# Half of q as a pair of seven products, the first pair's weights in places of their own, and a third group ahead of the last heads

## The chip, the cores and the metric

One Trainium2 chip, of which the kernel uses one core. The metric is the device time of one execution in microseconds. The engines are called as in the profile: PE (TensorE: matmuls, with PEld for its weight loads), DVE (VectorE), ACT (ScalarE), POOL (GpSimd) and SP (SyncE, which only issues DMAs). Each works through its own instructions in order; instructions on different engines meet through semaphores.

## What is computed

One layer of an encoder on 1024 tokens of 1024 channels, all in float32. The input is normalised, then one projection of 1024 x 5120 gives eight parts:

```python
h = layer_norm(x, emb_ln_g, emb_ln_b)
q, k, v, z_a, u, z_b, g_a, g_b = split(h @ w_in)          # 4 x 512, 2 x 512, 2 x 1024
attn = neighbourhood_attention(q, k, v, rpb)              # 8 heads of 64, window 8 x 16 on a 16 x 64 grid
y_a = attn * silu(z_a)
u = centred_depthwise_conv(u, conv_w, conv_b)
y_b = (rg_lru(u, forward) + rg_lru(u, backward)) * silu(z_b)
m = sigmoid(g_a + b0) * (y_a @ w_ba) + sigmoid(g_b + b1) * (y_b @ w_bb)
out = layer_norm(ALPHA * h + m @ w_out)
```

## The kernel before

**Products in three parts.** Every float32 operand of a matmul is split into a high half (rounded to the type that PE takes) and a low half (the rest). `mm3` (line 122) makes a product of three matmuls for each piece of 128 of the inner dimension: high x high, low weight x high, high weight x low. The high half is a copy, mostly on ACT, the low half a difference (`lo_of`, line 119) on DVE or POOL.

**Stage 1, lines 369 to 559.** Eight tiles of 128 tokens are loaded, normalised, turned by PE (`tile_in`) and split into the four blocks B11, B12, B21, B22 (inner dimension by token half). v is computed tile by tile (`v_part`, `v_hi`, `v_lo`, `v_store`). For the later tiles (4 to 7) the sums T1 to T4 of blocks are formed: `t_full` (line 271: a copy t3 by ACT out of PSUM, then four differences on DVE), `t_last` (line 282, two more), `t_hi` (ACT) and `t_lo` (POOL).

**q, lines 508 to 582.** q has 512 channels, so four blocks m of 128, each in two token halves n. `q_part(m, n)` is a plain product of 24 matmuls; `qk_load` and `qk_prep` load and split its weights (high on ACT, low on POOL); `q_hi`, `q_lo`, `q_store` scale it by 0.125, split it and send it to DRAM. (0, 0) and (1, 0) stand among the tiles; the other six run after the last v, in the loop of line 561. In that loop the weights of pair 0 are loaded (`s_load`), summed (`s_sum`, DVE) and split (`s_hi`, `s_lo`).

**The pair loop, lines 973 to 1001.** k, z_a, z_b, u, g_a and g_b are computed two blocks of 128 channels at a time: 16 pairs, each a 2 x 2 product of blocks in seven products of 12 matmuls (the sums a11, a12, s2, s1, s3, s4, a22 of weight blocks against B11, B21, T2, T1, T3, B22, T4) in place of eight. One product is a slot. In slot k of a pair the results of earlier products leave PSUM (`evacuate`, line 896: ACT's copies u1, u2, u3 and DVE's sums, through the `take_...` function of that pair), and one operand of the next pair is prepared. `at(slot, pos, f)` puts other work in slots by hand: the convolution stages at `CONV_AT`, two gate stages and a scan for each of four channel blocks at `GATE_AT`, the pools of the next stage at `LATE_AT` and `HEAD_AT`. PE gets four small matmuls of a gate stage in between. The decay rates (lines 594 to 612) are some 30 tiny steps on DVE ahead of the loop.

**Attention, lines 1145 to 1210.** Head by head scores, softmax and values, with the y_b branch product as filler matmuls.

**Merge and output, lines 1225 to 1339.** The y_a branch products (`b_group`, 12 matmuls for a group, three for each k, where k is a pair of heads) run slot by slot. The last pair of heads (k = 3) is finished late by `gated` (DVE, ACT, DVE). So the groups of slots 0 and 1 run their first three k, and the two fourths follow in slot 1. `merge` and `merge_lo` combine both branches and split the sum; then come the output products (`o_product`) and the last normalisation.

What sets the order: all five queues are written out by hand (`manual_schedule`), so the program's order is the order of each engine. Buffers of one tag are shared, and a new tile waits until the old one's readers are done.

Of the kernel before, what the change touches and what calls it, by code (L numbers as in the profile page):

```python
# [14 lines left out]
P = 128  # L15
# [51 lines left out]
def encoder_kernel(ctx, tc, x, gb1, gb, w_qk, w_v, w_s, w_ba, w_bb, w_gate, smalls, bias, w_out, out):  # L67
# [35 lines left out]
    V.memset(eps_z[:], EPS * TWICE * TWICE)  # L103
    smh = cst.tile([P, SM_N], F32, name="smh")
    warm = cst.tile([P, 1], F32, name="warm")
# [13 lines left out]
    def lo_of(eng, lo, full, hi):  # L119
        eng.tensor_tensor(lo, full, hi.bitcast(F32), ALU.subtract)  # L120
# [119 lines left out]
    def keep(i):  # L240
        SP.dma_start(h_d[i], xs[i][:])
# [12 lines left out]
    def tp4(i, kk):  # L254
        return tps[i, kk][:].rearrange("p (k t) -> p k t", k=4)
# [12 lines left out]
    def f(t, i):  # L268
        return t[:, :, ti(i)].bitcast(F32)

    def t_full(i):

        for c, tag in ((1, "a21"), (2, "a12"), (3, "a22")):
            tt[i, c] = wsp.tile([P, 4, P], F32, tag=tag, bufs=2 if c == 3 else 1, name=f"t{c}_{i}")
        t1, t2, t3 = (tt[i, c][:] for c in (1, 2, 3))
        A.copy(t3, tp4(i, 0))
        V.tensor_tensor(t1, tp4(i, 0), f(B11[0], i), ALU.subtract)
        V.tensor_tensor(t1, t1, f(B11[1], i), ALU.subtract)
        V.tensor_tensor(t2, tp4(i, 1), t1, ALU.subtract)
        V.tensor_tensor(t3, tp4(i, 1), t3, ALU.subtract)  # L280
# [6 lines left out]
    def t_hi(i, *cs):  # L287
        for c in cs:
            A.copy(Ts[c][0][:, :, ti(i)], tt[i, c][:])
# [53 lines left out]
    def s_load(p, *names):  # L343
        for o in names if p < N_PAIR else ():
            t = wsp.tile([P, 4, P], F32, tag=o, bufs=2 if o == "a22" else 1, name=f"{o}_{p}f")
            SP.dma_start(t[:], w_s[p, ("a11", "a21", "a12", "a22").index(o)])
            s_a[p, o] = t

    def s_sum(p, *names):
        for o in names if p < N_PAIR else ():  # L350
            a, b, op = dict(s1=("a21", "a22", ALU.add), s2=("s1", "a11", ALU.subtract),
                            s3=("a11", "a21", ALU.subtract), s4=("a12", "s2", ALU.subtract))[o]
            t = s_a[p, o] = wsp.tile([P, 4, P], F32, tag=o, name=f"{o}_{p}f")
            V.tensor_tensor(t[:], s_a[p, a][:], s_a[p, b][:], op)
# [141 lines left out]
    keep(5)  # L496
    qk_load(2)
    tile_in(4)
    tile_lo(4)
    ln_next(7)  # L500
    t_full(4)
    v_part(3, "a", KS)
# [14 lines left out]
    t_lo(4, 4)  # L517
    keep(7)
    q_part(1, 0)
    t_full(5)  # L520
    q_hi(1, 0)
# [37 lines left out]
    v_store(7)  # L559
    s_load(0, "a11")  # L560
    for m in range(4):
        for n in BOTH if m > 1 else (1,):
            q_part(m, n)
            if m < 2:
                qk_prep(m + 2)
                if m == 0:
                    qk_load(3)
                    t_hi(7, 2, 1, 3)
                    t_lo(7, 2, 1, 3)
                    t_last(7)  # L570
                    t_hi(7, 4)
                    t_lo(7, 4)
                    s_load(0, "a21", "a22", "a12")
                else:
                    s_sum(0, "s1", "s2", "s3", "s4")
            q_hi(m, n)
            q_lo(m, n)
            q_store(m, n)
            if m > 1:
                for w in (OPS[:2], OPS[2:4], OPS[4:6], OPS[6:])[2 * (m - 2) + n]:  # L580
                    s_hi(0, w)
                    s_lo(0, w)
    s_load(1, "a11", "a21", "a12", "a22")
    for pl in (ln, wpl, hb12, pst, ps0):
        pl.release()
# [7 lines left out]
    nsp = lru.tile([P, 8], F32, name="nsp")  # L593
    t0, t1, t2 = (lru.tile([P, 8], F32, name=f"sp{c}") for c in range(3))
    lam = sm[:, SM_LAM:SM_LAM + 8]
    V.tensor_scalar(smh[:], sm[:], 0.5, None, ALU.mult)
    V.tensor_scalar(t0[:], lam, -1.0, None, ALU.mult)
    V.tensor_tensor(t0[:], lam, t0[:], ALU.min)
    A.activation(t0[:], t0[:], AF.Exp)
    V.tensor_scalar(t1[:], t0[:], 2.0, None, ALU.add)  # L600
    V.reciprocal(t1[:], t1[:])
    V.tensor_tensor(t0[:], t0[:], t1[:], ALU.mult)
    V.tensor_tensor(t1[:], t0[:], t0[:], ALU.mult)
    V.tensor_scalar(t2[:], t1[:], 1.0 / 21.0, 1.0 / 19.0, ALU.mult, ALU.add)
    for n in (17, 15, 13, 11, 9, 7, 5, 3, 1):
        V.tensor_tensor(t2[:], t2[:], t1[:], ALU.mult)
        V.tensor_scalar(t2[:], t2[:], 1.0 / n, None, ALU.add)
    V.tensor_tensor(t2[:], t2[:], t0[:], ALU.mult)
    V.tensor_scalar(t0[:], lam, -1.0, 0.0, ALU.mult, ALU.max)
    V.scalar_tensor_tensor(t0[:], t2[:], 2.0, t0[:], ALU.mult, ALU.add)  # L610
    V.tensor_scalar(sp[:], t0[:], C_LRU, None, ALU.mult)
    V.tensor_scalar(nsp[:], t0[:], -C_LRU, None, ALU.mult)

# [36 lines left out]

    def take_k(m0):

        def consume(mi, n, add, o, c=None):
            c = o if c is None else c
            if add is not None:
                V.tensor_tensor(c[:], add[:], o[:], ALU.add)
            tag, w = ("uc", S) if (mi, n) == (1, 1) else ("up", S + 3)
            t = lru.tile([P, w], F32R, tag=tag, bufs=2, name=f"k{m0}{mi}{n}")
            hi, lo = t[:, :HALF], t[:, HALF:S]

            def high():
                A.copy(hi, c[:])

            def store():
                lo_of(V, lo, c[:], hi)
                SP.dma_start(k_d[m0 + mi][:, :, halves[n]], t[:, :S].rearrange("p (z f) -> p z f", z=2).bitcast(F32))
            return [high, store]
        return consume
# [134 lines left out]

    late, b_w, heads = {}, {}, {}

# [62 lines left out]
    def gates_a(j):  # L868
        return lambda: take_zg(ga_d, 2 * j, "ga", SM_BM)

    def gates_b(j):
        return lambda: take_zg(gb_d, 2 * j, "gb", SM_BM + 8)

    takes = [lambda: take_u(0), lambda: take_zg(zb_d, 0, "zb"), lambda: take_zg(za_d, 0, "za"), gates_a(0), gates_a(1),
             lambda: take_u(2), gates_b(0), lambda: take_zg(zb_d, 2, "zb"), gates_a(2), gates_b(1),
             lambda: take_k(0), gates_a(3), lambda: take_k(2), lambda: take_zg(za_d, 2, "za"), gates_b(2), gates_b(3)]
# [354 lines left out]
    for slot in range(2 * NK + 2):  # L1231
        j, n = divmod(slot, 2)
        if 1 < slot <= 2 * NK:
            merge(*divmod(slot - 1, 2), sums_m[slot - 1])
        if slot == 2:
            at0.release()
            mlp = pool("mlp")
            ml.update({(j, n): mlp.tile([P, HALF], F32R, name=f"ml{j}{n}") for j in range(NK) for n in range(2)})
            wo += [pair(mlp, [P, D], f"wo{k}") for k in range(NK - 2, NK)]
        for q in (0, 1) if slot == 2 else (slot - 2,) if slot > 3 else ():  # L1240
            merge_lo(*divmod(q, 2), sums_m.pop(q))
        if slot == 2:
            pst.release()
            banks[0] = tc.alloc_tile_pool(name="ps8", bufs=8, space=bass.MemoryType.PSUM, reuse_waits="tile")
        if j < NK:
            if n == 0:
                b_load(0, j + 2)
            g_load(0, j + 1, n, **(dict(tag=f"u{slot % 4}", bufs=1) if slot % 4 else dict(tag="z", bufs=5)))
            o = sums_m[slot] = pst.tile([P, HALF], F32, tag="mb", bufs=2, name=f"mb0{n}") if slot < 2 else bank(f"mb{j}{n}")
# [6 lines left out]
            if n == 0 and j > 0:  # L1256
                b_split(0, j + 1, A)
# [168 lines left out]
```

## Time and profile before

| | us |
|---|---|
| median of 3 runs | 686.44 |
| lowest, highest | 683.94, 686.56 |
| profiled execution, its time | 684.15 |
| profiled execution, its span | 682.4 |
| mean granted TensorE clock | 0.996 |

The span goes from the first to the last instruction. In the tables of stretches and in the order of time, each row begins with microseconds from the span's start. "idle before" is the time that an engine stood before an instruction, with what ended it. A matmul of 512 columns is shown with its duration of 0.39 us, but one starts every 0.227 us. The lines themselves stand in the prediction.

### The profile page before, as it was taken

What the parts mean: (1) busy time and instruction counts of PE and PEld (TensorE: products, weight loads), DVE (VectorE), ACT (ScalarE), POOL (GpSimd) and SP (SyncE); (2) the same over time, 40 slices, a digit from 0 to 9 for tenths busy, and PEclk for the clock granted to TensorE, in tenths of its full rate; (3) what the DMA queues carried; (4) which work ended last, traced back from release to release, by engine and by line L of the source; (5) the groups of instructions that cost most, each with busy time, mean ns of one, the idle gap of its engine ahead of it and who ended that gap; (6) DMA issues with size and microseconds to landing.
All of it is one profiled execution on the core that took longest, in us unless ns stands there. A gap on an engine that the chain in (4) does not pass through costs nothing.

```text
span 682.4 us, 9299 instructions
## 1 busy us (share of the span) xinstructions
PE 666.3 (98%) x3177; PEld 555.0 (81%) x3177; DVE 495.0 (73%) x821; ACT 364.0 (53%) x612; POOL 353.8 (52%) x258
## 2 busy tenths in 40 slices
PE   8999999999999999999999999999999999999995
PEld 6787888888888888888788888888888878888884
DVE  7866766796899599879977785377788777533434
ACT  4553524247686677768576635477777544310110
POOL 5697451344576577567647534115255446435442
PEclk9999999999999999999999999999999999999998
DMA  8754164233424133531453457898794557512211
GB/s 314 241 187 154 63 233 169 78 92 124 124 93 147 68 109 110 183 124 47 170 198 114 174 175 262 293 371 304 257 322 141 179 192 279 183 62 93 92 62 61
DMA packets 48702, 113.39 MB, mean 166 GB/s; under 512 B 5056, under 2 KB 9744, under 8 KB 47120
## 3 DMA queue, kind: packets, MB, share of 16 engines
q1 hardware_dynamic: 48624, 112.81, 47.6%
q8 instruction: 25, 0.41, 0.2%
q14 instruction: 21, 0.17, 0.1%
q10 hardware_dynamic: 32, 0.01, 0.0%
HBM read 77.11 MB, written 35.68 MB: 165 GB/s over the span
## 4 chain that ended last, share of the span: by engine, by line
PE 81%; DVE 8%; DMA 4%; POOL 3%; ACT 1%; issue 1%; SPq 1%; DVEq 0%; POOLq 0%; ACTq 0%
PE a L126 29%; PE o L126 13%; PE s L126 11%; PE mb L126 10%; PE q L126 5%; PE acc L1077 3%; PE s L1031 3%; PE pt L1053 2%; POOL x L238 2%; PE v L303 2%; PE g L729 2%; DMA wvsl<-in_w_v_dram 1%; DMA ks<-k_d 1%; DVE ws_l L120 1%; DVE uc L687 1%
## 5 line engine op out<-in xcount | busy, mean ns | idle before, releaser
L126 PE MATMUL o<-wo_h,ml 128*128 128x512 f32 (+1 forms) x136 | 51.2, 377 | 0.0
L126 PE MATMUL o<-wo_l,mh 128*128 128x512 f32 (+1 forms) x136 | 51.2, 376 | 0.0
L126 PE MATMUL o<-wo_h,mh 128*128 128x512 f32 (+1 forms) x136 | 51.2, 376 | 0.0
L126 PE MATMUL a<-ht_h,ws_h 128*128 128x512 f32 x128 | 50.0, 390 | 0.0
L126 PE MATMUL a<-ht_h,ws_l 128*128 128x512 f32 x128 | 49.8, 389 | 0.0
L126 PE MATMUL a<-ht_l,ws_h 128*128 128x512 f32 x128 | 49.8, 389 | 0.0
L126 PE MATMUL a<-b_h,wa_h 128*128 128x512 f32 x128 | 49.8, 389 | 0.0
L126 PE MATMUL a<-b_h,wa_l 128*128 128x512 f32 x128 | 49.8, 389 | 0.0
L126 PE MATMUL a<-b_l,wa_h 128*128 128x512 f32 x128 | 49.8, 389 | 0.0
L1041 DVE CUSTOM_DVE_ANT_0 sc<-s,bias 128x384 f32<-128x384 f32 (+1 forms) x64 | 33.4, 522 | 22.4 <-PE s L1031 14.0
L1316 DVE SCALAR_TENSOR_TENSOR z<-z,o 128x512 f32<-128x512 f32 (+1 forms) x17 | 11.2, 656 | 51.1 <-PE o L126 51.1
L1061 ACT CAST pt_h<-pt 128x384 fp32r<-128x384 f32 x64 | 29.0, 454 | 25.8 <-PE pt L1053 17.9
L1326 POOL TENSOR_TENSOR z<-z,gb 128x1024 f32<-128x1024 f32 x7 | 16.8, 2396 | 48.7 <-ACT z L1325 48.7
L1046 ACT ACTIVATE p<-sc,summ 128x384 f32<-128x384 f32 (+1 forms) x64 | 37.8, 591 | 5.2 <-DVE summ L1041 5.0
L1295 ACT ACTIVATE sd<-mv,eps_z 128x1 f32<-128x1 f32 x8 | 2.4, 294 | 67.1 <-DVE mv L1321 67.1
L303 PE MATMUL v<-wv,b_h 128*128 128x512 f32 x128 | 32.8, 398 | 2.7 <-ACT b_h L258 1.6
L120 DVE TENSOR_TENSOR pt_l<-pt,pt_h 128x384 fp32r<-128x384 f32 x64 | 33.2, 519 | 2.1 <-ACT pt_h L1061 1.6
L1031 PE MATMUL s<-ks,qs 128*128 128x384 f32 (+1 forms) x128 | 31.3, 326 | 0.5 <-DMA ks<-k_d 0.5
L837 POOL CAST wb_h<-wb 128x512 fp32r<-128x512 f32 x9 | 7.0, 780 | 47.5 <-DMA wb<-in_w_bb_dram 29.6
L303 PEld LDWEIGHTS v<-wv,b_h 128*128 128x128 f32 x128 | 23.6, 188 | 9.2 <-ACT b_h L258 2.3
L120 POOL TENSOR_TENSOR wb_l<-wb,wb_h 128x512 fp32r<-128x512 f32 x16 | 22.2, 1388 | 16.4 <-ACT wb_h L835 15.6
L1053 PEld LDWEIGHTS pt<-ident,p 128*128 128x128 f32 x176 | 23.1, 140 | 8.6
(438 smaller groups left out, 2201.3 us busy)
## 6 DMA issues: line engine op xcount, KB each, us to landing
ks<-k_d SPq DMA_DIRECT2D x8, 1024.0 KB, 8.0
h_d<-x SPq DMA_DIRECT2D x8, 512.0 KB, 4.5
v_d<-vs SPq DMA_DIRECT2D x8, 512.0 KB, 4.0
q_d<-q SPq DMA_DIRECT2D x8, 512.0 KB, 3.0
ga_d<-ga SPq DMA_DIRECT2D x16, 256.0 KB, 2.0
gb_d<-gb SPq DMA_DIRECT2D x16, 256.0 KB, 2.1
k_d<-k SPq DMA_DIRECT2D x8, 512.0 KB, 4.0
qs<-q_d SPq DMA_DIRECT2D x8, 512.0 KB, 5.5
```

What stands on the lines that cost most here:

```text
L120: eng.tensor_tensor(lo, full, hi.bitcast(F32), ALU.subtract)
L126: PE.matmul(o, a, b, start=first and i == 0, stop=last and i == len(prods) - 1, skip_group_check=not (first and last))
L238: G.tensor_tensor(z[:, halves[c]], z[:, halves[c]], gb_t[w][c][:], op)
L303: PE.matmul(vos[i][:], a, wv[kind == "w"][k][:], start=vn[i] == 0, stop=vn[i] == 23)
L729: PE.matmul(o[:, n, :], w[:, 2 * d + b, :], us[b][:, n * HALF:(n + 1) * HALF], start=z == 0, stop=z == 1)
L1031: PE.matmul(o[:, :P * len(near(t))], q[:, t * P:(t + 1) * P], k[:, z, keys], start=z == 0, stop=z == 1)
L1041: V.tensor_tensor_reduce(s[:, :w], o[:, :w], heads[h][2][:, b0:b0 + w], -1.0, 3.0e38, ALU.add, ALU.min, accum_out=sums[h][0][:, t:t + 1])
L1046: A.activation(probs[h % 2][t][:], scs.pop((h, t))[:, :w], AF.Exp, bias=sums[h][0][:, t:t + 1], scale=-1.0, accum_out=sums[h][1][:, t:t + 1])
L1053: PE.transpose(tp[:, n * P:(n + 1) * P], probs[h % 2][t][:, z * P:(z + 1) * P], ident[:])
L1061: A.copy(pt[0][:, span(b)], tps[h, b][:, :P * len(near(b))])
L1077: PE.matmul(acc[g][:, d:d + w], vvs[h // 2][:, b, h % 2, :], pt[:, a:a + w], start=b in (1, 6) and z == 0, stop=z == 1 and b == (4, 7)[g])
L1326: G.tensor_tensor(z[:], z[:], gb2[:, 0, :], ALU.mult)
```

## The change

1. The blocks m = 2 and 3 of q are no longer plain products. They become a seventeenth pair, in place 14 of the loop, so the loop has seven slots more; `take_k` becomes `take_qk`, which can scale. All later places in slots move.
2. Pair 0's weights are loaded by a new `s_first`, earlier, into buffers of the input tiles and of q's weights instead of buffers that v's weights and the tiles' sums use. Its sums and splits stand beside q(0, 1) and q(1, 1), the low half of a11 on DVE instead of POOL; the splits of s3 and s4 come in slots 1 to 3 of the loop. ACT's copy t3 is a function of its own (`t_copy`), for tile 7 ahead of `t_last(6)`.
3. The decay rates become a generator, `decay_rates`, of which a part runs in each of the slots 1 to 8.
4. In the merge stage three groups (slots 0, 1, 2) run their first three k, and the three fourths follow in slot 2. The third group uses a PSUM buffer of the scores.

```diff
-N_PAIR = 16
+N_PAIR = 17
+RATES_AT = range(1, 9)
-CONV_AT = (7, 24, 45, 66)
-GATE_AT = (14, 24, 35, 45, 56, 66, 77, 87)
-LATE_AT = (102, 102, 103, 104, 105)
-HEAD_AT = 109
+CONV_AT = (7, 25, 47, 69)
+GATE_AT = (14, 25, 36, 47, 58, 69, 80, 92)
+LATE_AT = (109, 109, 110, 111, 112)
+HEAD_AT = 116
...
+    def t_copy(i):
+        tt[i, 3] = wsp.tile([P, 4, P], F32, tag="a22", bufs=2, name=f"t3_{i}")
+        A.copy(tt[i, 3][:], tp4(i, 0))
...
+    def s_first():
+
+        for pl, tag, bufs, names in ((ln, "x", 5, ("a11", "a12")), (wpl, "ws", 1, ("a21", "a22"))):
+            t = pl.tile([P, 2, 4, P], F32, tag=tag, bufs=bufs, name=f"{names[0]}_0f")
+            for c, o in enumerate(names):
+                SP.dma_start(t[:, c], w_s[0, ("a11", "a21", "a12", "a22").index(o)])
+                s_a[0, o] = t[:, c]
...
-            lo_of(G if o in LO_POOL else V, lo[:], s_a[p, o][:], hi[:])
+            lo_of(G if o in LO_POOL[p == 0:] else V, lo[:], s_a[p, o][:], hi[:])
...
-    qk_load(2)
...
     keep(7)
+    s_first()
     q_part(1, 0)
...
+    t_copy(6)
     t_full(6)
     t_hi(6, 2, 1, 3)
     t_lo(6, 2, 1, 3)
+    t_copy(7)
+    t_last(6)
     v_hi(5)
+    t_hi(6, 4)
+    t_lo(6, 4)
     v_lo(5)
     v_store(5)
-    t_last(6)
-    t_hi(6, 4)
-    t_lo(6, 4)
...
-    s_load(0, "a11")
-    for m in range(4):
-        for n in BOTH if m > 1 else (1,):
-            q_part(m, n)
...
+    q_part(0, 1)
+    t_hi(7, 2, 1, 3)
+    t_lo(7, 2, 1, 3)
+    t_last(7)
+    s_hi(0, "a11")
+    t_hi(7, 4)
+    t_lo(7, 4)
+    s_lo(0, "a11")
     s_load(1, "a11", "a21", "a12", "a22")
+    q_hi(0, 1)
+    q_lo(0, 1)
+    q_store(0, 1)
+    q_part(1, 1)
+    s_hi(0, "a12")
+    s_lo(0, "a12")
+    s_sum(0, "s1", "s2")
+    s_hi(0, "s2")
+    s_lo(0, "s2")
+    s_hi(0, "s1")
+    s_lo(0, "s1")
+    s_sum(0, "s3", "s4")
+    s_hi(0, "a22")
+    s_lo(0, "a22")
+    q_hi(1, 1)
+    q_lo(1, 1)
+    q_store(1, 1)
...
+    for slot, o in enumerate(("s3", "s4"), 1):
+        at(slot, 1, lambda o=o: s_hi(0, o))
+        at(slot + 1, 0, lambda o=o: s_lo(0, o))
+    for slot in RATES_AT:
+        at(slot, 1, lambda: next(rates, None))
...
-            run(b_group(0, j, n, ya, o, range(3 if slot < 2 else 4)))
-            if slot == 1:
+            run(b_group(0, j, n, ya, o, range(3 if slot <= 2 else 4)))
+            if slot == 2:
+                for c in range(3):
+                    run(b_group(0, c // 2, c % 2, ya, sums_m[c], range(3, 4)))
+                    if c == 1:
+                        b_split(0, 2, A)
                 for c in range(2):
-                    run(b_group(0, 0, c, ya, sums_m[c], range(3, 4)))
-                merge(0, 0, sums_m[0])
+                    merge(0, c, sums_m[c])
```

More of the change, by code (lines that the diff above doesn't have):

```diff
@@ L103, in encoder_kernel @@
     V.memset(eps_z[:], EPS * TWICE * TWICE)
-    smh = cst.tile([P, SM_N], F32, name="smh")
+    smh = cst.tile([P, 2 * NK], F32, name="smh")
     warm = cst.tile([P, 1], F32, name="warm")
@@ L500, in encoder_kernel @@
     ln_next(7)
+    t_copy(4)
     t_full(4)
@@ L518, in encoder_kernel @@
     keep(7)
+    s_first()
     q_part(1, 0)
+    t_copy(5)
     t_full(5)
@@ L802, in gate_stage @@
                 at(slot + 12 + n, 0, lambda n=n: gated(n))
-    late, b_w, heads = {}, {}, {}
+    late, b_w, heads, rates = {}, {}, {}, decay_rates()
     def late_pools():
@@ L1232, in encoder_kernel @@
         j, n = divmod(slot, 2)
-        if 1 < slot <= 2 * NK:
+        if 2 < slot <= 2 * NK:
             merge(*divmod(slot - 1, 2), sums_m[slot - 1])
[L1235 to L1240, printed above, removed]
+        for q in (2, 3) if slot == 4 else (slot - 2,) if slot > 5 else ():
             merge_lo(*divmod(q, 2), sums_m.pop(q))
-        if slot == 2:
+        if slot == 4:
             pst.release()
```

105 lines of the change are left out of this document (52 added, 53 removed).

## The prediction

> **What bounds the kernel now.** I read the page first (span, busy times, the chain of waits), then the table of stretches, the list of who waited for whom, and last the order of time on single engines around the three places that the diff touches.
>
> ```profile
> span 682.4 us, 9299 instructions
> PE 666.3 (98%) x3177; PEld 555.0 (81%) x3177; DVE 495.0 (73%) x821; ACT 364.0 (53%) x612; POOL 353.8 (52%) x258
> PE 81%; DVE 8%; DMA 4%; POOL 3%; ACT 1%; issue 1%; SPq 1%; DVEq 0%; POOLq 0%; ACTq 0%
> ```
>
> TensorE works through 666.3 of 682.4 us and carries 81% of the chain. So a matmul that goes is worth its whole pitch, and any work moved beside TensorE is free only until TensorE has to wait for it. Where does it wait today?
>
> ```profile
> 66.00:77.00 11.00, 11.00 (x49) 9.08 (x50) 8.04 (x12) 5.12 (x10) 5.12 (x5) 1.00 0.27 97
> 77.00:88.00 11.00, 11.00 (x50) 9.13 (x49) 7.60 (x10) 4.81 (x8) 8.21 (x6) 1.00 0.35 116
> 88.00:110.00 22.00, 22.00 (x99) 18.22 (x98) 13.80 (x16) 7.71 (x14) 7.38 (x5) 1.00 0.59 205
> 110.00:129.00 19.00, 19.00 (x86) 15.56 (x85) 17.27 (x50) 4.74 (x9) 6.17 (x7) 1.00 0.46 154
> 300.00:330.00 30.00, 29.63 (x131) 23.97 (x130) 29.86 (x28) 22.76 (x28) 22.66 (x15) 1.00 0.23 82
> 536.00:548.00 12.00, 10.34 (x57) 8.55 (x56) 8.73 (x13) 4.93 (x10) 4.24 (x3) 1.00 0.77 279
> PE mb L126 <- ACT ya_h L1122: 1.7, 1, 1.7
> PE a L126 <- DVE w L762: 0.4, 1, 0.4
> ```
>
> The columns of the first six rows are the length, then the busy time of PE, PEld, DVE, ACT and POOL, the granted clock, and the share and rate of the DMAs. From the last v to the end of the first pair (66 to 129) TensorE has no gap at all. In the pair loop it has one of 0.4 us, where VectorE is full (29.86 of 30). Near the last heads it stands 1.7 us. Those are the places to look at.
>
> **The removed products.** Six halves of q run today between these two instructions:
>
> ```profile
> 76.99 0.39 PE L126 MATMUL q<-b_h,wqk_h 128*128 128x512 f32 x1
> 109.63 0.39 PE L126 MATMUL a<-b_h,wa_h 128*128 128x512 f32 x1
> 109.80 8.16 PE a L126 x36
> ```
>
> That is 144 matmuls in 32.64 us, a pitch of 0.2267 us; the pair loop has the same pitch (36 in 8.16 us). Four halves of 24, so 96 matmuls, become seven products of 12, so 84. Twelve fewer are 12 x 0.2267 = **-2.72 us**. The pair adds to VectorE nine instructions that make its operands and three sums of its evacuation (the four differences of q are there before and after), 12 x 0.68 = 8.2 us, and to GpSimd five casts and two low halves. They lie beside its own 19 us of TensorE, in slots 91 to 107, where no convolution and only the last gate stage runs; I cost them at nothing, and without that cover they would be those 8.2. The loads are the same 1 MB.
>
> **The first pair's operands.** This is where the cover goes. Before, 144 matmuls lay between the last v and the first product; now 48 do, so q ends at 76.99 + 48 x 0.2267 = 87.87, and the second matmul of product a11, which needs the low half of its weight, is due at 88.10. That low half is now VectorE's, and it is queued behind t_last(7). The rows that set it:
>
> ```profile
> 74.73 1.66 ACT L289 CAST ht_h<-t 128x512 fp32r<-128x512 f32 x3 [2.61 <-DVE t L279]
> 75.43 4.25 POOL L120 TENSOR_TENSOR ht_l<-t,ht_h 128x512 fp32r<-128x512 f32 x3 [3.88 <-ACT ht_h L289]
> 78.57 1.66 DVE L285 TENSOR_TENSOR t<-t,b_l 128x512 f32<-128x512 f32 x1
> 80.96 1.30 POOL L120 TENSOR_TENSOR ht_l<-t,ht_h 128x512 fp32r<-128x512 f32 x1 [1.28 <-ACT ht_h L289]
> 82.99 0.69 DVE L279 TENSOR_TENSOR t<-tp,t 128x512 f32<-128x512 f32 x1
> 83.77 2.41 POOL L120 TENSOR_TENSOR wqk_l<-wqk_s,wqk_h 128x1024 fp32r<-128x1024 f32 x1 [1.51 <-ACT wqk_h L164]
> 86.12 4.25 POOL L120 TENSOR_TENSOR ht_l<-t,ht_h 128x512 fp32r<-128x512 f32 x3
> 87.46 1.76 DVE L284 TENSOR_TENSOR t<-b_h,t 128x512 f32<-128x512 f32 x1 [1.99 <-POOL ht_l L120]
> 89.26 1.66 DVE L285 TENSOR_TENSOR t<-t,b_l 128x512 f32<-128x512 f32 x1
> ```
>
> Tile 6's t_last ends at 80.23 as before (it follows GpSimd's three low halves, which do not move). v_hi(5) and v_lo(5) are now behind it; their bank goes to q(1, 1), due at 76.99 + 24 x 0.2267 = 82.43, and is free at 80.9. So VectorE does v_lo(5), then the four steps of t_full(7). Their second step reads two tiles of SBUF and so, as I read these rows, gets through only when GpSimd's instruction at 80.96 is over (82.26). The third step then ends at about 83.5 instead of 83.68: copying t3 earlier buys almost nothing, since v_lo(5) takes its place. ACT's high half follows, and GpSimd starts 0.70 us after ACT (74.73 to 75.43), so at 84.3; before, it stood behind q's weights (83.77 + 2.41) until 86.12. From GpSimd's start to the end of t_last(7) there are 4.80 us (86.12 to 90.92), so t_last(7) ends at 89.1 and the low half of a11 at 89.8 (0.68 more). TensorE stands from 88.10 to 89.8: **+1.7 us**. From below 1.2, if v_lo(5) slips in without cost. From above 2.8: t_copy(7) may have to wait until GpSimd has read tile 6's t3 (79.68), v_hi(5) and t_hi(6, 4) are queued behind it on ACT, and all that follows comes 0.5 later, with as much again for waits that I do not see.
>
> After that VectorE works without a rest. Up to the low half of s3 it has 13 instructions of the size of the rows below (two of q, nine of pairs 0 and 1, the first u, s3 itself), three small ones of the decay rates, and about 1.3 us of waits for ACT, whose q_hi(0, 1) is queued behind t_hi(7, 4).
>
> ```profile
> 93.73 2.75 DVE L354 TENSOR_TENSOR s_0f<-a_0f 128x512 f32<-128x512 f32 x1 [0.94 <-DMA a_0f<-in_w_s_dram]
> 97.13 0.68 DVE L354 TENSOR_TENSOR s_0f<-a_0f 128x512 f32<-128x512 f32 x1
> 97.73 0.68 DVE L354 TENSOR_TENSOR s_0f<-a_0f,s_0f 128x512 f32<-128x512 f32 x1
> 98.25 1.32 POOL L120 TENSOR_TENSOR wa_l<-a_0f,wa_h 128x512 fp32r<-128x512 f32 x1 [2.31 <-ACT wa_h L359]
> 121.45 1.63 POOL L359 CAST ws_h<-s_1f 128x512 fp32r<-128x512 f32 x2 [2.00 <-DVE s_1f L354]
> ```
>
> At the pitch of 0.60 (97.13 to 97.73) that is 89.8 + 13 x 0.60 + 0.6 + 1.3 = 99.5. TensorE needs it 48 matmuls after the second one of a11, at 89.8 + 10.9 = 100.7. But GpSimd has two low halves (1.3 each) and one cast (0.8) in that time, and the sum at 93.73 shows what that can do: 2.75 instead of 0.68 us. So s3 is ready between 99.5 and 102.9, and TensorE waits 0 to 2.2; I take half of GpSimd's 3.4, so 101.2 and **+0.5 us**. [...]
>
> The decay rates, before in one block whose last 28 steps run from the first row here to the second, go into slots 1 to 8:
>
> ```profile
> 112.91 0.17 DVE L600 TENSOR_SCALAR sp<-sp 128x8 f32<-128x8 f32 x1 [0.28 <-ACT sp L599]
> 119.80 0.16 DVE L612 TENSOR_SCALAR nsp<-sp 128x8 f32<-128x8 f32 x1
> ```
>
> They took 6.9 us while TensorE had all of pair 0 ready. Spread, they are at most five a slot, 1.2 of 2.72 us, and from slot 4 on VectorE's work (1.4 to 2.0 us a slot) fits. What they delay is pair 1's operands, due a whole pair later. The four loads of pair 0 move on SP's queue from behind v_store(7) to behind keep(7), past q_store(1, 0) and four v_stores: four issues, at a time when the DMAs are 0.27 to 0.35 busy (66 to 88) and v's stores still wait for v. s_load(1) comes ahead of q's stores, and its third load waits for t_lo(7, 4), about 91.2; behind it waits q_store(0, 1), which the heads alone read. Nothing of this is on the path; the 0.94 us that the first sum waited for a load goes, off the path too.
>
> **The timetable of the loop.** Convolution and gate stages move by 0 to 5 slots. VectorE's 29.86 of 30 us is the stretch in which pair 10's k meets the last convolution. With the new slots that convolution's steps start at 70 instead of 67, beside k's (71 to 78), while the scan before it is one slot clear of it. I take **+0.3 us**, between -0.4 (today's gap goes) and +2.
>
> **The tail.**
>
> ```profile
> 541.05 0.40 PE L126 MATMUL mb<-ya_h,wb_h 128*128 128x512 f32 x1
> 543.22 1.75 POOL L120 TENSOR_TENSOR wb_l<-wb,wb_h 128x512 fp32r<-128x512 f32 x1
> 545.63 0.44 PE L126 MATMUL mb<-ya_l,wb_h 128*128 128x512 f32 x1
> 547.06 0.62 ACT L1122 CAST ya_h<-attn 128x512 fp32r<-128x512 f32 x1 [2.11 <-DVE attn L1120]
> 547.73 0.50 PE L126 MATMUL mb<-ya_h,wb_h 128*128 128x512 f32 x1 [1.66 <-ACT ya_h L1122]
> 547.71 0.69 DVE L120 TENSOR_TENSOR ya_l<-attn,ya_h 128x512 fp32r<-128x512 f32 x1 [0.68 <-ACT ya_h L1122]
> 548.45 0.50 PE L126 MATMUL mb<-ya_l,wb_h 128*128 128x512 f32 x1
> ```
>
> Today 21 matmuls run from 541.05 to 545.86, then TensorE stands until ya_h of the last half is cast. The new third group has nine more that need only the first three k: 30 run to 547.9, by then ya_h is there (547.68) and ya_l (548.40) nearly. Its weight's low half ends at 544.97, before slot 2 starts (545.2). What stays is a wait of some 0.1. Pause and second wait were 1.87 + 0.2; I take **-2.0 us**, between -2.1 and -0.9. The merges start when ya_l lets them, as before, and at three instructions of 0.69 to a slot of 2.72 us VectorE's backlog is gone long before the output products.
>
> **Sum.** -2.72 + 1.7 + 0.5 + 0.3 - 2.0 = -2.2 us on a span of 682.4, so 680.2; the profiled execution took 684.15, 1.75 more than its span, and would take 681.95. The runs shown have a median of 686.44, 2.3 above that execution, so I forecast 684.2.
>
> **Rivals.** First, *everything is in time*: the low half of a11 and s3 cost 0.3 together, and -2.72 - 2.0 + 0.3 = -4.4 gives 682.0. For it speaks that the loads come 20 us earlier and GpSimd loses 4.8 us of q's weights; against it the 4.80 us that tile 7 needs after GpSimd's start. Second, *slower*: in slots 70 to 80 VectorE falls more than one slot (2.72 us) behind, ACT stands in its order before the square root that waits for VectorE's product, and the copies that free a bank of PSUM come late behind it. The price is the convolution's VectorE work if none of it is covered: three steps of 1.39 and two of 1.36.
>
> ```profile
> L687 DVE SCALAR_TENSOR_TENSOR uc<-up,sm,uc 128x1024 f32<-128x1024 f32 x12 | 16.7, 1390 | 1.7 <-ACT uc L683 1.7
> L120 DVE TENSOR_TENSOR us<-uc,us 64x1024 fp32r<-64x1024 f32 x8 | 10.9, 1362 | 0.3
> ```
>
> That is 6.9, so with the other terms -2.5 + 6.9 = +4.4 and 690.8. Against it: the stretch was full before and cost 0.4. Third, *the third group gains nothing*, because another wait follows where the first went (the bank, or the first half's ya_l): -2.2 + 2.0 = -0.2 in all, 686.2.
>
> **Chances.** Forecast 0.57, all in time 0.20, slower 0.09, no gain at the tail 0.14. The range must hold the first rival's 682.0 less some noise and the third's upper side: 681.4 to 687.9; the unknown costs alone give -4.8 + 1.2 - 0.4 = -4.0 to -3.6 + 2.8 + 2.2 + 2 = +3.4. A measurement of this kernel tells about 0.5% (3.4 us) from no change. Faster by more: most of the first rival and a little of the forecast, 0.22; slower by more: the second, 0.08; within: 0.70.
>
> **What would show it.** The first product of pair 0 starts with one matmul, then a gap of about 1.7 us that ends with VectorE's low half; a second gap before s3 of at most 2; a pair stage of 119 products; no wait for ya_h. It is wrong if the first gap is missing or above 3 us, if the loop has gaps of more than 1 us, or if the wait for ya_h stays.

## The result, and the profile after

The changed kernel takes 690.56 us (median of 6 executions, 689.39 to 691.21); the kernel before, run beside it, 686.35. The ratio is 1.0070, with a 95% interval of 1.0056 to 1.0084: slower by 0.7%, where the prediction had 0.3% faster and a range that ends at 687.9.

The page of the changed kernel (its profiled execution took 691.21), the same three lines as before:

```profile
span 689.4 us, 9306 instructions
PE 669.0 (97%) x3165; PEld 553.3 (80%) x3165; DVE 501.5 (73%) x834; ACT 364.9 (53%) x615; POOL 349.2 (51%) x262
PE 81%; DVE 7%; POOL 4%; ACT 3%; DMA 2%; issue 2%; SPq 1%; DVEq 0%; POOLq 0%; ACTq 0%
```

The twelve matmuls are gone (3177 to 3165 on PE), and yet PE is busy 2.7 us longer. So the loss is not only waiting: the matmuls themselves take longer, in part by a slower clock (below). The table of stretches, columns as in the prediction:

```profile
66.00:77.00 11.00, 10.14 (x48) 8.17 (x47) 8.64 (x13) 5.25 (x11) 5.07 (x4) 1.00 0.68 216
77.00:88.00 11.00, 11.00 (x49) 9.00 (x48) 8.49 (x10) 5.61 (x12) 6.75 (x5) 1.00 0.19 64
88.00:110.00 22.00, 17.56 (x75) 13.50 (x75) 20.20 (x38) 8.66 (x16) 10.90 (x10) 1.00 0.50 163
536.00:548.00 12.00, 12.00 (x78) 10.46 (x77) 8.80 (x20) 7.61 (x18) 3.19 (x4) 1.00 0.35 120
```

The last row ends about where the merge stage begins here, at 547.05; from there to the output products the trace shows no wait on PE, so the one for ya_h is gone. The stretch from 88 to 110 had no gap before. Now PE is idle for 4.4 of 22 us in it, and VectorE, at 13.8 before, is at 20.2. Where PE waits there, in order of time:

```profile
89.89 0.39 PE L127 MATMUL a<-b_h,wa_h 128*128 128x512 f32 x1
92.23 0.50 PE L127 MATMUL a<-b_h,wa_l 128*128 128x512 f32 x1 [1.95 <-DVE wa_l L121]
98.20 0.50 PE L127 MATMUL a<-ht_h,ws_h 128*128 128x512 f32 x1 [0.45 <-ACT u L945]
105.99 0.50 PE L127 MATMUL a<-ht_h,ws_h 128*128 128x512 f32 x1 [2.04 <-ACT u L949]
```

The first gap is the predicted one: one matmul of a11, then a wait for VectorE's low half. The other two wait for ScalarE's copies of a11's bank (u1 and u2 of `evacuate`), not for the low half of s3. Next, how long each stage takes, from the start of its first matmul to that of the next stage's (us, from the order of time on PE). The columns to the right of "after" are runs of the experiments:

| stage | before | after | before, smh small | after, smh wide | before, third group | last order |
|---|---|---|---|---|---|---|
| up to q(0, 1) | 76.99 | 78.85 | 77.36 | 77.44 | 76.99 | 78.51 |
| q, then to the first product | 32.64 | 11.04 | 33.08 | 10.88 | 32.64 | 10.88 |
| pairs | 320.54 | 345.71 | 321.14 | 345.78 | 320.48 | 341.42 |
| attention | 110.88 | 111.45 | 110.92 | 111.15 | 110.76 | 110.93 |
| merge | 45.85 | 44.73 | 46.47 | 44.08 | 43.84 | 43.82 |
| output to the end | 95.5 | 97.6 | 97.4 | 95.7 | 95.5 | 95.6 |

A seventeenth pair is 84 x 0.2267 = 19.04 us, so the pairs took 6.1 more than the prediction's pitch gives them. Of these, 4.9 are the three waits above, counted from start to start beyond a pitch. The output stage, which the change does not touch, took 2.1 more. Each group of its matmuls, before and after (mean ns of one last):

```profile
L126 PE MATMUL o<-wo_h,mh 128*128 128x512 f32 x120 | 46.7, 389 | 0.0
```

```profile
L127 PE MATMUL o<-wo_h,mh 128*128 128x512 f32 x120 | 47.2, 394 | 0.0
```

One starts every 0.2327 us in place of 0.2267 (60 in 13.96 us in place of 13.60), at a granted clock of 1.00. Last, the changed kernel's profiled execution lost 1.9 us before q(0, 1), in a stretch in which the clock was granted at 0.66:

```profile
15.00:20.00 5.00, 4.87 (x17) 3.70 (x18) 2.91 (x6) 1.58 (x4) 3.33 (x3) 0.66 0.68 266
```

(1 - 0.66) x 5 = 1.7 us. The profiled execution of before has 1.00 there. Just ahead of this stretch PE waited 0.73 us at 13.4 and 0.70 at 15.1; in before the two waits are 0.74 and 0.38.

### The profile page after: what moved, and what is told of

Its sections match the earlier page's. It is cut to its first block, busy times and chain, and to the rows that moved or that the text cites. A ratio compares the mean times of both kernels' runs of the same rounds, so it can differ in the third digit from the quotient of the medians.

```text
span 689.4 us, 9306 instructions
## 1 busy us (share of the span) xinstructions
PE 669.0 (97%) x3165; PEld 553.3 (80%) x3165; DVE 501.5 (73%) x834; ACT 364.9 (53%) x615; POOL 349.2 (51%) x262
## 4 chain that ended last, share of the span: by engine, by line
PE 81%; DVE 7%; POOL 4%; ACT 3%; DMA 2%; issue 2%; SPq 1%; DVEq 0%; POOLq 0%; ACTq 0%
PE a L127 31%; PE o L127 13%; PE mb L127 13%; PE s L127 12%; PE acc L1114 4%; PE s L1068 3%; POOL x L239 3%; PE pt L1090 3%; PE g L760 2%; DMA wvsl<-in_w_v_dram 1%; DVE t L288 1%; DVE b_l L121 1%; DVE t L289 1%; DVE s_0f L366 1%; POOL ht_l L121 1%
## 5 line engine op out<-in xcount | busy, mean ns | idle before, releaser
L127 PE MATMUL a<-ht_h,ws_h 128*128 128x512 f32 x136 | 53.3, 392 | 2.5 <-ACT u L949 2.0
L127 PE MATMUL a<-b_h,wa_l 128*128 128x512 f32 x136 | 53.0, 390 | 2.0 <-DVE wa_l L121 2.0
L127 PE MATMUL a<-ht_l,ws_h 128*128 128x512 f32 x136 | 53.0, 390 | 0.0
L127 PE MATMUL a<-b_h,wa_h 128*128 128x512 f32 x136 | 53.0, 390 | 0.0
L127 PE MATMUL a<-b_l,wa_h 128*128 128x512 f32 x136 | 53.0, 389 | 0.0
L127 PE MATMUL a<-ht_h,ws_l 128*128 128x512 f32 x136 | 52.9, 389 | 0.0
L127 PEld LDWEIGHTS a<-ht_h,ws_h 128*128 128x128 f32 x136 | 25.5, 188 | 8.7 <-ACT u L949 2.5
L127 PEld LDWEIGHTS a<-b_h,wa_l 128*128 128x128 f32 x136 | 25.5, 188 | 7.7 <-DVE wa_l L121 2.4
```

Source lines behind the costliest of these rows:

```text
L127: PE.matmul(o, a, b, start=first and i == 0, stop=last and i == len(prods) - 1, skip_group_check=not (first and last))
```

## The experiments

### The place of the tiles

The diff has a line that the prediction passed over: the tile of halved biases, smh, shrinks from 60 columns (240 bytes a partition, kept as 256) to 16 (64 bytes). It is one of the first tiles on the left side of SBUF, so everything behind it there, B11, B21, B22, the sums T, the pair loop's weights, the merged operand of the output products, moves by 192 bytes. What lies on the right side (q's weights, the gates' operands, six of the eight blocks of wo) stays.

```diff
-    smh = cst.tile([P, SM_N], F32, name="smh")
+    smh = cst.tile([P, 2 * NK], F32, name="smh")
```

*smh_wide* takes this line back in the changed kernel (the 16 columns are written and read as in the change):

> The changed kernel with one thing undone: the small constant tile smh is 60 columns wide again (16 of them are written and read), so every left-hand tile of SBUF lies where it lay before the change. Theory 'places': in the changed kernel's trace an output matmul has a pitch of 0.2323 us against 0.2267 before at a granted clock of 1.00, because the tiles' places moved; with the old places the pitch is 0.2267 again, the 420 matmuls of the output stage take 2.1 us less, and with 1 to 2 us from the other stages the kernel takes 686.5 to 688.5 in place of 690.6. Rival 'execution': the pitch differs from one execution to another whatever the places; 690.6 +- 0.7, and the output stage's pitch is either.

*before_smh_small* puts it alone into the kernel before:

> The kernel before with that one thing of the change alone: smh 16 columns wide. Theory 'places': the output stage's pitch rises from 0.2267 to about 0.2323, and the time from 686.4 to 688.5 to 690. Rival 'execution': 684 to 686.5 as before, pitch 0.2267 in an execution that takes 684.

smh_wide: 686.74 us, ratio to the kernel before 1.0014 (1.0003 to 1.0025), so 3.8 us of the loss are gone. before_smh_small: 689.45, ratio 1.0057 (1.0037 to 1.0078), so 3.9 us lost by a tile of 192 bytes less. The output group of smh_wide, then that of before_smh_small:

```profile
L127 PE MATMUL o<-wo_h,mh 128*128 128x512 f32 x120 | 46.7, 389 | 0.0
```

```profile
L126 PE MATMUL o<-wo_h,mh 128*128 128x512 f32 x120 | 47.2, 393 | 0.0
L126 PE MATMUL q<-b_h,wqk_h 128*128 128x512 f32 x64 | 25.3, 395 | 0.0
L126 PE MATMUL a<-ht_l,ws_h 128*128 128x512 f32 x128 | 49.9, 390 | 0.0
```

Theory "places" holds both ways. The other two rows say which matmuls suffer: q (a block of the left side by weights of the right side) goes from 390 to 395 ns, while a product of the pairs, whose operands both lie on the side that moved, is at 390 against 389. So what counts, by these rows, is not where one tile lies but how the two lie to each other. The output stage says the same within one trace: in the changed kernel its matmuls start every 0.2333 us with the first six blocks of wo and every 0.2300 with the last two, which lie on the left and moved too (0.2267 with all eight in the kernel before). Why the last two are not back at 0.2267 stays open. *before_smh_24*, *before_smh_32* and *before_no_smh* move the tiles by other amounts (24 columns: 160 bytes; 32: 128; none, with the halves written over sm: 256):

```diff
-    smh = cst.tile([P, SM_N], F32, name="smh")
...
-    V.tensor_scalar(smh[:], sm[:], 0.5, None, ALU.mult)
+    V.tensor_scalar(sm[:, SM_BM:], sm[:, SM_BM:], 0.5, None, ALU.mult)
```

(In the other two, `smh = cst.tile([P, 24], ...)` and `[P, 32]`.)

> The kernel before with smh 24 columns wide, so that the left-hand tiles move by 160 bytes in place of the 192 of 16 columns. If any other place than the old one costs: pitch of the output matmuls above 0.230 and 688 to 690. If the place within 64 bytes decides (160 puts the tiles at a multiple of 64, the old place and 192 do not): pitch 0.2267 or less, 684 to 686.5.

> The kernel before with smh 32 columns wide: the left-hand tiles move by 128 bytes (16 columns: 192, 24 columns: 160; both cost 4 to 7 us). If the place within 128 bytes decides: pitch of the output matmuls 0.2267 as before, 684 to 686.5. If any other place than the old one costs: pitch 0.232 or more, 688 to 692.

> The kernel before without the tile smh at all (the halves are written over the same columns of sm): the left-hand tiles move by 256 bytes. Moves of 128, 160 and 192 bytes gave pitches of 0.2318, 0.2332 and 0.2326 in the output stage against 0.2267. If the place within 256 bytes decides: 0.2267 again and 684 to 686.5. If any other place than the old one costs: 0.231 or more and 688 to 690.

Times: 691.69 (ratio 1.0105, 1.0092 to 1.0119), 688.86 (1.0058, 1.0038 to 1.0078) and 685.29 (1.0006, 0.9992 to 1.0021). Their output groups, in this order:

```profile
L126 PE MATMUL o<-wo_h,mh 128*128 128x512 f32 x120 | 47.5, 395 | 0.0
```

```profile
L126 PE MATMUL o<-wo_h,mh 128*128 128x512 f32 x120 | 47.2, 394 | 0.0
```

```profile
L125 PE MATMUL o<-wo_h,mh 128*128 128x512 f32 x120 | 46.7, 389 | 0.0
```

A move by 256 bytes costs nothing that these runs can tell; 128, 160 and 192 cost. So the theories that a place within 64 bytes or within 128 decides both fall. The place within 256 bytes decides, for this kernel's tiles and of the moves tried. Why was not tested and stays open.

### The third group alone

*tail_only* is the kernel before with hunk 4 of the change and nothing else.

> The kernel before with the third group ahead of the last heads alone. By the prediction's term: 2.0 less, so 684.4, with TensorE's idle time between the last heads and the output products gone (it was 1.87 + 0.2). By the changed kernel's trace, where the stage took 1.1 less and not 2.0: 685.3. Rival 'nothing gained': 686.4, with another wait in the place of that for ya_h.

681.96 us, all six executions between 681.20 and 682.62; ratio 0.9945 (0.9928 to 0.9962). The merge stage takes 43.84 in place of 45.85: 2.0 less, the predicted term, and the stretch has no gap:

```profile
536.00:548.00 12.00, 12.00 (x66) 10.09 (x64) 8.68 (x12) 5.22 (x11) 4.24 (x3) 1.00 0.78 285
```

But the median fell by 4.0 (from 685.94), more than was expected by any of the three. Against the kernel before's profiled execution (684.15) it is 2.2, about the gap alone; the rest fits the clock. The kernel before's wait of 1.66 us for ya_h is followed by a slow stretch in some executions and not in others; here is one where it is (before_smh_24):

```profile
550.52 0.50 PE L126 MATMUL mb<-ya_h,wb_h 128*128 128x512 f32 x1 [1.66 <-ACT ya_h L1122]
...
552.07 0.63 PE L126 MATMUL mb<-ya_h,wb_l 128*128 128x512 f32 x1
552.50 0.63 PE L126 MATMUL mb<-ya_l,wb_h 128*128 128x512 f32 x1
```

```profile
550.00:555.00 5.00, 4.48 (x12) 3.23 (x13) 4.27 (x7) 2.90 (x5) 0.00 (x0) 0.66 0.61 221
```

A matmul starts every 0.43 us there instead of every 0.227. Of the five profiled executions with this wait, three have the stretch: those with smh of 24 and of 32 columns and the one without smh, but not the one with 16, nor that of the kernel before. So for the kernel before itself the stretch is inferred from its times, and they agree: of its 87 executions beside the experiments, the 34 with a mean granted clock up to 0.994 take 685.2 to 689.0 us; the 50 from 0.996 on take 682.7 to 685.6, but for one at 686.4; the three between lie at 685.2 to 687.0. So a gap on TensorE has two prices here: its length, and about 1.7 us in the executions in which the clock drops behind it.

In the traces of this study, waits of 1.65 to 2.3 us on TensorE had such a stretch behind them in six of fifteen cases.

### The waits of the first pair

*rates_late* moves the decay rates in the changed kernel (`RATES_AT = range(6, 14)`).

> The changed kernel with the decay rates' eight parts in slots 6 to 13 in place of 1 to 8. Theory 'Exp in the way': the third gap of the first pair (2.2 us before s3) comes from the copy of a11's sum, which stands on ScalarE behind the rates' Exp, which waits 3.6 us for VectorE; with the Exp later the copy runs at about 103.0 and the gap falls to 0.3 or less: 690.6 - 2.0 = 688.6. Rival 'VectorE late': the gap is s3's own low half or sum on a VectorE that is behind anyway; the gap stays at 1.5 to 2.2 and the time at 690 to 690.6.

Why this one? In the changed kernel the copy that PE waits for at 105.99 stands on ScalarE behind the rates' Exp, and the Exp waits for three small steps at the end of VectorE's queue:

```profile
102.80 0.57 DVE L619 TENSOR_TENSOR sp<-sm,sp 128x8 f32<-128x8 f32 x1
```

```profile
103.45 1.28 ACT L620 ACT_TABLE_LOAD   x1 [3.63 <-DVE sp L619]
104.74 0.21 ACT L620 ACTIVATE sp<-sp 128x8 f32<-128x8 f32 x1
104.86 0.60 ACT L371 CAST ws_h<-s_0f 128x512 fp32r<-128x512 f32 x1
105.36 0.58 ACT L949 COPY u<-a 128x512 f32<-128x512 f32 x1
```

In rates_late the copy runs as soon as PE has finished the sum, and the gap before s3 is gone. Then a new one stands in pair 1, where the rates now meet the first convolution on VectorE (first ScalarE's, then PE's row):

```profile
100.71 0.59 ACT L949 COPY u<-a 128x512 f32<-128x512 f32 x1 [0.47 <-PE a L127]
```

```profile
129.73 0.50 PE L127 MATMUL a<-ht_h,wa_h 128*128 128x512 f32 x1 [1.83 <-DVE c L662]
```

689.74 us, where 688.6 was expected. That is 0.8 less than the changed kernel, which the intervals of the two ratios (1.0038 to 1.0076 and 1.0056 to 1.0084) do not tell from nothing. The cause of the gap was right, the expected gain was not: the stall moved. The other attempts start from smh_wide, so that places play no part. Its first gap is 2.2 us long and followed by the slow clock:

```profile
90.93 0.79 PE L127 MATMUL a<-b_h,wa_l 128*128 128x512 f32 x1 [2.22 <-DVE wa_l L121]
```

```profile
90.00:95.00 5.00, 4.07 (x11) 3.26 (x12) 3.70 (x7) 2.42 (x5) 1.29 (x1) 0.66 0.50 186
```

*a11_early* and *rates_early*:

```diff
+    s_hi(0, "a11")
     v_hi(7)
     v_lo(7)
     v_store(7)
+    s_lo(0, "a11")
...
     t_last(7)
-    s_hi(0, "a11")
     t_hi(7, 4)
     t_lo(7, 4)
-    s_lo(0, "a11")
```

> smh_wide (686.7) with both halves of a11's weight ahead of tile 7's last steps: the cast before v_hi(7) on ScalarE, the low half before t_last(7) on VectorE. Theory 'next in line': the first gap (2.2 us, behind wa_l of a11) goes, but t_last(7) still ends at about 90.2 and the low half of a12, which stands behind it and behind q's, is done at about 92.8 where TensorE now needs it at 91.3; a gap of some 1.4 comes there, and the kernel gains 0.5 to 1: 685.7 to 686.2. Rival 'the gap goes': 2.2 less, 684.5, with no new wait above 0.5 us. The wait for the copy of a11's sum (1.45) stays in both.

```diff
-RATES_AT = range(1, 9)
+RATES_AT = range(4, 7)
...
     tile_lo(5)
+    next(rates)
...
+    next(rates)
     tile_lo(6)
...
+    next(rates)
     v_lo(4)
...
+    next(rates)
+    next(rates)
     t_last(6)
```

> smh_wide with the decay rates taken out of the first pair: five of the eight parts (the Exp among them) in gaps of VectorE between tile 5 and tile 7's v, three in slots 4 to 6; their scratch lies in smh's spare columns. Theory 'Exp and small steps in the way': the wait for the copy of a11's sum (1.45 us before s3) goes to 0.3 or less, and nothing takes its place later, as it did with the rates in slots 6 to 13 (1.83 before a product of pair 1): 686.7 - 1.2 to 1.7 = 685.0 to 685.5. Rival 'VectorE late anyway': a wait of 1 us or more stays before s3 or s4, 686 to 686.7.

Both were expected to gain and got slower than smh_wide, whose interval is 1.0003 to 1.0025: 687.93 (ratio 1.0053, 1.0039 to 1.0066) and 688.01 (1.0055, 1.0041 to 1.0069). In a11_early the first gap went, and the wait came back one product later, as a gap of 1.26 + 0.39 before a12; then 1.22, then 2.04 with the slow clock behind it (the copies u1 and u2):

```profile
92.35 0.50 PE L127 MATMUL a<-b_h,wa_h 128*128 128x512 f32 x1 [1.26 <-ACT wa_h L371]
93.25 0.50 PE L127 MATMUL a<-b_h,wa_l 128*128 128x512 f32 x1 [0.39 <-DVE wa_l L121]
```

In rates_early the wait before s3 went as expected, but two parts of the rates came to stand on VectorE where the changed kernel has GpSimd's three low halves of tile 6 (77.17 to 81.41). Three steps of 128 x 8 took 1.1 to 1.2 us there, those behind them 0.17. That GpSimd held them up is inferred from the place. They made t_last(6), at 81.65 (78.50 in the changed kernel), and with it all of tile 7, later, so the first gap grew from 2.2 to 3.3:

```profile
77.49 1.14 DVE L206 TENSOR_TENSOR smh<-smh 128x8 f32<-128x8 f32 x1
78.67 1.22 DVE L207 TENSOR_SCALAR smh<-smh 128x8 f32<-128x8 f32 x1
79.92 1.21 DVE L206 TENSOR_TENSOR smh<-smh 128x8 f32<-128x8 f32 x1
81.16 0.17 DVE L207 TENSOR_SCALAR smh<-smh 128x8 f32<-128x8 f32 x1
```

```profile
93.30 0.54 PE L127 MATMUL a<-b_h,wa_l 128*128 128x512 f32 x1 [3.34 <-DVE wa_l L121]
```

*all_early* has both, and t_last(7) behind the first operands:

```diff
+    s_lo(0, "a11")
+    s_hi(0, "a12")
+    s_lo(0, "a12")
+    s_sum(0, "s1", "s2")
+    s_hi(0, "s2")
+    s_lo(0, "s2")
...
+    s_hi(0, "s1")
+    s_lo(0, "s1")
     t_last(7)
     t_hi(7, 4)
     t_lo(7, 4)
```

> smh_wide with both of these and with t_last(7) behind the first operands: on VectorE come the low halves of a11 and a12, the sums s1 and s2 and their low halves, q's low half, and only then t_last(7) (its product a22 is the last of the pair). Theory: all three gaps of the first pair (2.2 + 0.4 + 1.45 in smh_wide) are below 0.5 together and nothing else comes: 686.7 - 3.7 = 683.0; against the kernel before with the third group alone (682.0) the pair of seven should then still gain 2.72, so 679.3 if smh_wide's dip of the granted clock at 90 us (5 us at 0.66, 1.7 us) hangs on the gap. Rival 'VectorE is full': a wait of 1 us or more for a22's or s3's operands; 684 to 686.

689.35 (ratio 1.0076, 1.0062 to 1.0090), one gap only, and the longest: 4.6 us before s2. The copy u1 (99.24) stood on ScalarE behind tile 7's high half, which waited for the t_last(7) that had been put behind everything:

```profile
97.71 0.62 ACT L323 CAST ht_h<-t 128x512 fp32r<-128x512 f32 x1 [2.28 <-DVE t L319]
98.23 0.61 ACT L401 CAST wa_h<-a_0f 128x512 fp32r<-128x512 f32 x1
98.75 0.59 ACT L363 ACTIVATE q<-q 128x512 fp32r<-128x512 f32 x1
99.24 0.57 ACT L958 COPY u<-a 128x512 f32<-128x512 f32 x1
```

### Can the first pair be fed at all?

Four more orders, each of which takes the gaps of the one before at their source. The edits are shown in part; the expectations name the rest (where the rates go, the order of pair 1's loads, and which engine makes the low halves of s3 and s4).

```diff
+    s_hi(0, "a11")
     q_part(0, 1)
     t_hi(7, 2, 1, 3)
     t_lo(7, 2, 1, 3)
+    s_lo(0, "a11")
+    v_hi(7)
+    v_lo(7)
+    v_store(7)
+    s_hi(0, "a12")
+    s_lo(0, "a12")
+    s_sum(0, "s1", "s2")
...
+    def last_steps():
+        t_last(7)
+        t_hi(7, 4)
+        t_lo(7, 4)
+        s_load(1, "a12")
+
+    at(1, 0, last_steps)
```

> The changed kernel with the tiles in their old places (smh 60 wide), the rates' first part with its Exp before tile 4's last steps and the other seven in slots 3 to 9, and the first pair in another order: low half of a11 right behind t_full(7), then v_lo(7), a12, the sums s1 and s2, q's two, s3 and s4; t_last(7) with its halves in slot 1, behind the copy of a11's sum. Theory: no gap of the first pair is above 0.7 us, so there is no stretch at a granted clock of 0.66 behind one either; tail_only's 682.0 less 2.7 for the twelve matmuls, so 679.3 to 680.3, and all its executions within 1.5 us. Rival 'VectorE has too much to do here whatever the order': a gap of 1.5 us or more at another product of the first two pairs; 682 to 686.

690.41 (ratio 1.0066, 1.0048 to 1.0084). No gap before a11, a12 and s2, but 2.15 before s3 (u2 behind tile 7's high half) and 3.73 before a22. VectorE, which frees a22's bank, waited 1.44 us behind pair 1's late load of a12 and then did some 2.5 us of the rates' small steps ahead of the sum that frees it. The granted clock was about 0.66 for ten us from 110 on.

```diff
+    t_last(7)
     for pl in (ln, wpl, hb12, pst, ps0):
         pl.release()
...
     def last_steps():
-        t_last(7)
         t_hi(7, 4)
...
+    for o in ("s3", "s4"):
+        at(0, 1, lambda o=o: s_hi(0, o))
+        at(0, 1, lambda o=o: s_lo(0, o))
```

> first_pair_order with its two gaps (2.15 before s3, 3.73 before a22) taken at their sources: tile 7's t_last(7) on VectorE ahead of the pair and only its halves behind the copy of a11's sum; s3's and s4's casts in slot 0 and their low halves on GpSimd, which was idle from 95 to 101; pair 1's a11 and a22 loaded ahead of v's last store; the rates' seven parts in slots 5 to 11. Theory 'the pair can be fed if each operand is ready in the order of use': gaps of the first two pairs 1 us in all, none above 1, no stretch of the clock below 1.00 behind them; 680 to 682. Rival 'too much for 119 products' worth of cover': again 2 us or more somewhere before the third pair; 683 to 689.

689.56 (1.0074, 1.0059 to 1.0090): a gap of 2.29 before s2, since the moved casts of s3 and s4, which wait for VectorE, stood ahead of the copy u1; and 2.09 in pair 1, the rates against the convolution again.

```diff
     def last_steps():
+        for o in ("s3", "s4"):
+            s_hi(0, o)
+            s_lo(0, o)
         t_hi(7, 4)
...
+    def a12_next():
+        s_lo(1, "a12")
+        s_sum(1, "s4")
+
+    at(5, 0, a12_next)
```

> first_pair_order_2 with the sources of its two gaps moved again: s3's and s4's casts behind the copy of a11's sum (slot 1) instead of before it, so that no instruction that waits for VectorE stands ahead of that copy; the rates' small steps in gaps between tile 5 and tile 7 and four parts in slots 5, 6, 15 and 16, away from the first convolution; pair 1's low half of a12 and its sum s4, which wait for a late load, behind the sum that frees a22's bank. Theory 'the twelve matmuls are worth their 2.72 us once nothing waits': gaps below 1 us in all up to the third pair and no stretch of the clock at 0.66 there, 679.5 to 681.5, less than tail_only's 682.0. Rival 'the cover is too short': a gap of 1.5 us or more at a22 or in pair 1 again, 683 to 688.

687.72 (1.0033, 1.0019 to 1.0047): 0.69 before s3 and 2.53 before a22. GpSimd's cast of pair 1's a12 waited for its load, and the cast of s2 behind it kept VectorE from the sum that frees the bank (GpSimd's, then VectorE's rows):

```profile
104.79 0.61 POOL L401 CAST wa_h<-a_1f 128x512 fp32r<-128x512 f32 x1 [2.78 <-DMA a_1f<-in_w_s_dram]
```

```profile
107.23 1.06 DVE L121 TENSOR_TENSOR ws_l<-s_1f,ws_h 128x512 fp32r<-128x512 f32 x1 [4.67 <-POOL ws_h L401]
108.21 0.68 DVE L664 TENSOR_TENSOR up<-u,a 128x512 f32<-128x512 f32 x1
```

```diff
     def a12_next():
+        s_hi(1, "a12")
         s_lo(1, "a12")
         s_sum(1, "s4")
...
-        s_hi(*prep)
+        if prep != (1, "a12"):
+            s_hi(*prep)
```

> first_pair_order_3 with one instruction moved: pair 1's cast of a12 on GpSimd, which waits until 104.8 for its load and held up the casts of s2 and s1 behind it, and so VectorE and the sum that frees a22's bank (gap of 2.53), goes behind that sum. Theory 'the twelve matmuls are worth their 2.72 us once nothing waits': the gap at a22 falls below 0.7 us and no other of 1.5 us takes its place; 685.6 - 2 = 681 to 683 for the kernel, below the kernel before by 3 us or more. Rival 'the cover is too short': a gap of 1.5 us or more at another place, 684 to 688.

683.51, all twelve executions between 682.79 and 684.25; ratio 0.9974 (0.9959 to 0.9990). The waits went as expected, the time did not quite: 681 to 683 was expected. One wait of 0.68 is left up to the third pair, and the clock stays at 1.00 there:

```profile
101.25 0.50 PE L127 MATMUL a<-ht_h,ws_h 128*128 128x512 f32 x1 [0.68 <-ACT u L972]
```

So the rival "the cover is too short" falls. But what is won is small: from q(0, 1) to the first group after the pairs it takes 10.88 + 341.42 = 352.3 against 32.64 + 320.48 = 353.1 in tail_only, 0.8 less where twelve matmuls are 2.7. Most of the difference is in this wait and four short ones, at 126, 185, 188 and 331 us: 2.4 us in all beyond a pitch, where tail_only's pairs have 0.65. And the rates' parts among the tiles cost a wait of nearly 1 us in v, which tail_only does not have:

```profile
72.92 3.94 PE L337 MATMUL v<-wv,b_h 128*128 128x512 f32 x16 [0.96 <-ACT b_h L289]
```

On balance it is behind tail_only: its shortest execution is longer than tail_only's longest (682.62), though the intervals of the two ratios just touch (0.9928 to 0.9962 there). The best kernel of this study is the kernel before with the third group alone; it beats both kernels.

## Why the prediction was wrong

*The removed products, -2.72.* Right: 12 matmuls fewer on PE.

*The low half of a11, +1.7 (1.2 to 2.8).* Right in place and cause, 2.1 in size (one matmul at 89.89, the next at 92.23, less a pitch). In the changed kernel's profile the second step of t_full(7), with both inputs in SBUF, took 1.35 us in place of 0.69 (83.19 to 84.54) beside GpSimd's instruction from 82.69 to 83.99, while the first, with one input in PSUM (82.48), took 0.68. GpSimd's start to the end of t_last(7) took 4.8 us as worked out; the start came later because `v_hi(7)`, ahead of tile 7's high halves on ScalarE, waited 2.5 us for a store to free its buffer. The prediction left that wait out:

```profile
85.61 0.59 ACT L314 CAST vs<-v 128x512 fp32r<-128x512 f32 x1 [2.51 <-DMA v_d<-vs]
86.09 1.67 ACT L293 CAST ht_h<-t 128x512 fp32r<-128x512 f32 x3
```

*s3, +0.5 (0 to 2.2).* Wrong in the operand. VectorE did fall behind: the low half of s3 was done at 104.57, 0.55 after it was due, so alone it would have cost about what was forecast. But PE waited for ScalarE's copies, about 0.6 before s2 and 2.2 before s3, 2.8 in all. The step that failed is "What they delay is pair 1's operands, due a whole pair later", said of the decay rates. It counted their small steps on VectorE and forgot the one on ScalarE: in a queue that runs in order, an Exp that waits for VectorE (3.63 us at 103.45) hands VectorE's delay to the copy behind it (105.36). rates_late shows it: with the Exp later, the copy no longer waits for it, and the gap before s3 is gone.

*The timetable of the loop, +0.3 (-0.4 to 2).* Of the size: today's gap of 0.37 went, one of 0.28 came, and attention waits 0.8 once where it waited 0.5. (In smh_wide, three short waits from 187 to 334 cost 0.7 more than the two of before.) The second rival (slots 70 to 80) did not occur; the result came out on its side by other causes.

*The tail, -2.0.* Right: 2.0 in tail_only. In the changed kernel it is 1.1, as the stage pays for the places there (0.6 in before_smh_small); in smh_wide it is 1.8.

*What was not in the sum at all.* The largest part, 3.8 of the 4.2 us lost, is a line of the diff that looks like saved space. "That is 144 matmuls in 32.64 us, a pitch of 0.2267 us" was taken for a constant; here it depends on where the operands lie (0.2267 or 0.2327 in the output stage). Without that line the changed kernel stands at +0.14% (smh_wide), about 1 us slower where -2.2 was forecast. The waits of the first pair are most of the rest: 4.9 in place of 2.2 in the changed kernel, 4.0 in smh_wide. The forecast also priced a gap at its length alone. In smh_wide's profile the slow clock behind the first gap costs some 1.6 more; with the longer waits (1.8) and small losses elsewhere (some 1.5 in all) that makes the 4.9 between the 2.7 that this execution is slower than the one of before and the 2.2 faster of the forecast.

*The base.* The sum was made against an execution of 684.15 and carried over to a median of 686.44 by adding 2.3. By the split of the times above that difference was itself the tail's gap, through the clock: in tail_only, with the gap gone, the profiled execution (681.98) and the median (681.96) are the same. And the range was narrower than the prediction's own costs: +3.4 on 686.4 is 689.8, where it ended at 687.9.

## What to carry to other kernels

Read a diff for tiles that change size, too: here a matmul's pitch depended on where its operands lie (0.2267 or 0.2327 us), and a smaller constant tile ahead of everything else cost more than the edit was forecast to win (3.8 us against 2.2). Compare the mean duration of untouched matmuls before looking for waits. When work moves into a stretch with less cover, walk every queue there, not only the one with the most work: the small instruction that waits for the late engine stalls all that stands behind it, as the Exp did here (TensorE stood 2.04 us for the copy behind it). And a gap of 2 us on TensorE can be worth nearly twice its length, as the third group's was (2.0 us of the stage, 4.0 of the median).

## What had not been expected of the hardware

For this kernel's tiles, the place within 256 bytes of SBUF decided between 389 and 395 ns for a matmul of the output stage (389 when the tiles stay or move by 256 bytes, 393 to 395 when they move by 128, 160 or 192); the kernel before takes 0.6 to 1.1% more in the bad places. Of eighteen waits of 1.6 us or more on PE in these traces, from q(0, 1) to the output products, nine were followed by some 5 us at a granted clock of about 0.66 (ten behind the one of 3.73): all three above 3.3 us, six of the fifteen between 1.6 and 2.6. Behind single waits below 1.6 us the tables of stretches show none in that part (first_pair_order has one of 0.78 at 445.70 and a clock of 1.00 behind it). But two shorter waits close together may be enough: in the first v the changed kernel's profiled execution has the same stretch (0.66 from 15 to 20) behind waits of 0.73 and 0.70 us, at 13.4 and 15.1; in that of the kernel before the two are 0.74 and 0.38 and the clock is 1.00. Of the runs of the experiments, first_pair_order has the stretch there too (0.66), and before_no_smh, before_smh_32 and first_pair_order_2 to 4 have 1.00.
